# Column roll of an 8192 x 8192 matrix: two rows per engine and DMA in the first three eighths of the copy

## Chip, core and metric

The kernel runs on one core of a Trainium2 chip. The metric is the device time of one launch in microseconds (us); lower is better. Three timed runs of the kernel before gave 815.59, 817.35 and 817.82 us, median 817.35 us.

## The reference

```python
def setup_inputs():
    return {"x": np.random.randn(8192, 8192).astype(np.float32), "shift": 100}

def reference(x, shift):
    return np.roll(x, shift, axis=1)
```

Each row of 8192 float32 values (32 KiB) is rotated right by 100 columns. There is no arithmetic: 256 MiB are read and 256 MiB are written, and every output element is a copied input element. Column w of the output is column w - 100 of the input; the first 100 output columns come from the last 100 input columns.

## The kernel before

A row of the output is cut in two at column a = 256 (the shift 100 rounded up to 128, and one more 128). The columns from 256 on, 7936 values or 31,744 B of each row, are the body; the columns below 256 are the head.

**The body (L37 to L46)** goes from DRAM to DRAM with no stop on the chip. L34 and L35 view the 8192 rows as 128 blocks c of 64 rows; inside a block, engine index e (16 values) and row index j (4 values) name row 4e + j. One `dma_start` at L45 takes one block c and one j: 16 rows that lie four rows (128 KiB) apart, one for each of the 16 DMA engines, 496 KB in all. SP (`nc.sync`) starts at block 0 and goes up, j from 0 to 3. ACT (`nc.scalar`) starts at block 127 and goes down, j from 3 to 0. Both take a DMA in turn in the order of the program: the loop runs i from 0 to 63, so i is SP's block and 127 - i ACT's. In the last two rounds (i = 62 and 63) `parts` cuts every row in two halves, so that a DMA carries 248 KB.

After each i the name of its last DMA is put on the list `marks` (L46), 64 entries in all.

**The head (L63 to L97)** is done by POOL (`nc.gpsimd`) and DVE, in 16 tiles of 512 rows, four rows to each of 128 partitions. `fetch` (L72) issues a load from POOL and makes it wait for the landing of the fetch four before it in the list `chain`. A tile has three fetches: t, which holds 256 columns around the boundary between a row and the next for three of the four rows; and two smaller ones straight into h. DVE copies the two parts of t to their places in h (L87 and L90). When all fetches are issued, POOL issues the 16 stores of h (L94), 512 KB each. Store k is held until a DMA of the body has landed: the one in `marks` at 24 + 36k/15, rounded down, so the first store waits for i = 24 and the last for i = 60.

SP and ACT issue nothing but the body's DMAs. POOL's queue holds the fetches in order and behind them the stores. A body DMA adds 16 to one of eight semaphores, four of them SP's and four ACT's, which the tile framework hands out in turn; before it reuses one it waits for the DMA that used it last. The first four DMAs of a queue have no such wait.

Of the kernel before, what the change touches and what calls it, by code (L numbers as in the profile page):

```python
# [1 line left out]

# [4 lines left out]


@with_exitstack
def kernel(  # L10
    ctx: ExitStack,
    tc: tile.TileContext,
    x: bass.AP,
    shift: int,
    out: bass.AP,
):
    nc = tc.nc
    n_rows, n_cols = x.shape
    s = shift % n_cols
    a = -(-s // 128) * 128  # L20
    if 0 < a <= 384 and a + 128 <= n_cols:
        a += 128
    g = a - s
    P = nc.NUM_PARTITIONS
    engines = [nc.sync, nc.scalar]
    n_chunks = 16
    rows = n_rows // n_chunks

    xm = x.rearrange("(c e j) w -> c j e w", e=16, j=4)  # L34
    om = out.rearrange("(c e j) w -> c j e w", e=16, j=4)  # L35
    marks = []
    if a < n_cols:  # L37
        blocks = n_rows // 64
        mid = (a + n_cols) // 256 * 128
        for i in range(blocks // 2):  # L40
            parts = ((a, mid), (mid, n_cols)) if i >= blocks // 2 - 2 and a < mid else ((a, n_cols),)
            for j in range(4):
                for eng, c, q in ((engines[0], i, j), (engines[1], blocks - 1 - i, 3 - j)):
                    for lo, hi in parts:
                        ins = eng.dma_start(out=om[c, q, :, lo:hi], in_=xm[c, q, :, lo - s:hi - s])  # L45
            marks.append(getattr(ins, "ins", ins).name)  # L46
    if a == 0:
        return


    if a > 512:
        for i in range(n_chunks):
            r = slice(i * rows, (i + 1) * rows)
            nc.gpsimd.dma_start(out=out[r, :s], in_=x[r, n_cols - s:])
            if g > 0:
                nc.gpsimd.dma_start(out=out[r, s:a], in_=x[r, :g])
        return

    Q = 4  # L63
    n_st = n_rows // (P * Q)
    reads = ctx.enter_context(tc.tile_pool(name="reads", bufs=n_st))
    heads = ctx.enter_context(tc.tile_pool(name="heads", bufs=n_st))
    xt = x.rearrange("(k p q) c -> k p q c", q=Q, p=P)
    ot = out.rearrange("(k p q) c -> k p q c", q=Q, p=P)
    tiles = []
    chain = []  # L70

    def fetch(to, of):  # L72
        ins = nc.gpsimd.dma_start(out=to, in_=of, single_packet=True)  # L73
        ins = getattr(ins, "ins", ins)
        if len(chain) >= 4:
            tc.add_manual_dep(ins, chain[-4].name,
                              mybir.DependencyInfo(mybir.DependencyClass.Sync, mybir.DependencyReason.DATA))
        chain.append(ins)

    for k in range(n_st):  # L80
        t = reads.tile([P, Q - 1, a], x.dtype)
        h = heads.tile([P, Q, a], x.dtype)
        lead = bass.AP(tensor=x.tensor, offset=(k * P * Q + 1) * n_cols - s,
                       ap=[[Q * n_cols, P], [n_cols, Q - 1], [1, a]])
        fetch(t[:], lead)
        fetch(h[:, Q - 1, :s], xt[k, :, Q - 1, n_cols - s:])
        nc.vector.tensor_copy(h[:, :Q - 1, :s], t[:, :, :s])  # L87
        if g > 0:
            fetch(h[:, 0, s:], xt[k, :, 0, :g])
            nc.vector.tensor_copy(h[:, 1:, s:], t[:, :, s:])  # L90
        tiles.append(h)
    first, last = len(marks) * 3 // 8, len(marks) * 15 // 16
    for k, h in enumerate(tiles):
        ins = nc.gpsimd.dma_start(out=ot[k, :, :, :a], in_=h[:], single_packet=True)  # L94
        if marks and n_st > 1:
            tc.add_manual_dep(getattr(ins, "ins", ins), marks[first + (last - first) * k // (n_st - 1)],
                              mybir.DependencyInfo(mybir.DependencyClass.Sync, mybir.DependencyReason.DATA))  # L97


# [1 line left out]
_INS = ['x', 'shift']  # L101
_OUTS = [((8192, 8192), 'float32')]

_NUMBERS = {'shift': 100}


# [26 lines left out]
```

## Time and profile before

| | |
|---|---|
| median of three runs | 817.35 us |
| the profiled execution | 816.2 us |
| its span, first to last instruction | 814.4 us |
| body DMAs from SP and from ACT | 264 each: 248 of 496 KB, 16 of 248 KB |
| issue to landing, 496 KB | 12.7 us (median) |
| fetches of t, 384 KB, issue to landing | 29.5 us (median) |
| head stores, 512 KB, issue to landing | 21.1 us (median) |
| first and last head store issued | 327.7 and 779.4 us |
| last fetch issued | 281.5 us |

The span is what the profile covers; the device time is 1.8 us longer. In the queue lines q1 is SP's, q10 ACT's and q0 POOL's; the columns are packets, MB, and the time of the packets as a share of the span of 16 engines. GB/s counts each byte once, although a byte of the body is both read from and written to HBM. "Issue to landing" runs from the issue on the queue to the last engine's semaphore write. The lines of waits name who waited, for what, the total in us, the number of times and the longest. The clock column in the stretches is TensorE's and plays no part here.

### The profile page before, as it was taken

The numbers are of one execution on the slowest core, as the hardware profiler recorded it, in microseconds if no ns is written. First come the engines' busy times: TensorE is split into PE (matmuls) and PEld (weight loads), VectorE is DVE, ScalarE is ACT, GpSimd is POOL, SyncE is SP. The second block draws the span as 40 slices with busy tenths as digits, with TensorE's granted clock in tenths as the row PEclk, the third lists the DMA queues.
The fourth block names the chain that finished last, engine by engine and source line by source line (L and its number), as shares of the span: only waits on it lengthen the run. The fifth ranks groups of instructions, "written<-read, shape, count | busy, mean of one in ns | idle before, by whom it ended". The sixth has DMA issues, their size and how long they took to land.

```text
span 814.4 us, 689 instructions
## 1 busy us (share of the span) xinstructions
DVE 12.0 (1%) x32; POOL 41.2 (5%) x68
## 2 busy tenths in 40 slices
DVE  0000000000000000000000000000000000000000
POOL 1001001101001000000000000000000000000000
DMA  9999999999999999999999999999999999999998
GB/s 314 346 347 343 351 344 332 338 347 342 356 344 349 345 334 338 345 337 342 337 350 322 352 338 335 357 342 331 352 352 318 356 347 335 340 339 347 334 331 294
DMA packets 22277, 276.90 MB, mean 340 GB/s; under 512 B 9472, under 2 KB 9728, under 8 KB 13824
## 3 DMA queue, kind: packets, MB, share of 16 engines
q1 hardware_dynamic: 8448, 130.04, 46.8%
q10 hardware_dynamic: 8448, 130.04, 44.1%
q0 software_dynamic: 5376, 16.78, 8.1%
q14 instruction: 5, 0.04, 0.0%
HBM read 268.44 MB, written 268.44 MB: 659 GB/s over the span
## 4 chain that ended last, share of the span: by engine, by line
DMA 95%; ACTq 0%; issue 0%; POOLq 0%
DMA out_dram<-in_x_dram 95%; ACTq L45 0%; POOLq L128 0%; POOLq L94 0%
## 5 line engine op out<-in xcount | busy, mean ns | idle before, releaser
L94 POOL DMA_DIRECT2D out_dram<-h x16 | 11.4, 715 | 486.7 <-DMA out_dram<-in_x_dram 448.9
L73 POOL DMA_DIRECT2D h<-in_x_dram x32 | 17.5, 547 | 197.1 <-DMA t<-in_x_dram 165.0
L73 POOL DMA_DIRECT2D t<-in_x_dram x16 | 12.1, 759 | 54.9 <-DMA h<-in_x_dram 54.0
L87 DVE COPY h<-t 128x300 f32<-128x300 f32 x16 | 5.9, 367 | 287.3 <-DMA t<-in_x_dram 287.3
L90 DVE COPY h<-t 128x468 f32<-128x468 f32 x16 | 7.5, 468 | 0.0
L114 POOL MEMSET const-float32-0.0<- 128x1 f32 x1 | 0.1, 99 | 0.2 <-issue 0.2
L114 POOL MEMSET const-bfloat16-1.0<- 128x1 bf16 x1 | 0.1, 102 | 0.0
L114 POOL MEMSET const-float32-1.0<- 128x1 f32 x1 | 0.1, 99 | 0.0
L114 POOL MEMSET const-uint8-127<- 128x1 uint8 x1 | 0.1, 99 | 0.0
## 6 DMA issues: line engine op xcount, KB each, us to landing
out_dram<-in_x_dram SPq DMA_DIRECT2D x248, 496.0 KB, 12.7
out_dram<-in_x_dram ACTq DMA_DIRECT2D x248, 496.0 KB, 12.7
out_dram<-h POOLq DMA_DIRECT2D x16, 512.0 KB, 21.1
t<-in_x_dram POOLq DMA_DIRECT2D x16, 384.0 KB, 29.5
out_dram<-in_x_dram SPq DMA_DIRECT2D x16, 248.0 KB, 5.9
out_dram<-in_x_dram ACTq DMA_DIRECT2D x16, 248.0 KB, 5.9
h<-in_x_dram POOLq DMA_DIRECT2D x16, 78.0 KB, 24.3
h<-in_x_dram POOLq DMA_DIRECT2D x16, 50.0 KB, 21.2
```

Source lines behind the costliest of these rows:

```text
L73: ins = nc.gpsimd.dma_start(out=to, in_=of, single_packet=True)
L87: nc.vector.tensor_copy(h[:, :Q - 1, :s], t[:, :, :s])
L90: nc.vector.tensor_copy(h[:, 1:, s:], t[:, :, s:])
L94: ins = nc.gpsimd.dma_start(out=ot[k, :, :, :a], in_=h[:], single_packet=True)
L114: nc = _bacc.Bacc("TRN2", target_bir_lowering=False, num_devices=1)
```

## The change

For i below blocks * 3 // 16 = 24 (of 64) a DMA takes two values of j: its 16 engines each get two neighbouring rows, one after the other, 992 KB in all. There are then two DMAs of SP and two of ACT for an i, not four and four: 96 fewer over both queues. SP's rows keep their order (0 and 1, then 2 and 3). ACT takes the rows 2 and 3 of its block and then 0 and 1. `marks` still gets one entry for each i, and the rounds from i = 24 on, the head and its marks are as they were.

```diff
         for i in range(blocks // 2):
             parts = ((a, mid), (mid, n_cols)) if i >= blocks // 2 - 2 and a < mid else ((a, n_cols),)
+            if i < blocks * 3 // 16:
+                for j in (0, 2):
+                    for eng, c, q in ((engines[0], i, j), (engines[1], blocks - 1 - i, 2 - j)):
+                        ins = eng.dma_start(out=om[c, q:q + 2, :, a:].rearrange("j e w -> e j w"),
+                                            in_=xm[c, q:q + 2, :, a - s:n_cols - s].rearrange("j e w -> e j w"))
+                marks.append(getattr(ins, "ins", ins).name)
+                continue
             for j in range(4):
                 for eng, c, q in ((engines[0], i, j), (engines[1], blocks - 1 - i, 3 - j)):
                     for lo, hi in parts:
```

## The prediction

> **What bounds the kernel now.** I read the sections on slices and queues of the page first, then the chain, then the waits of SP's queue, then busy shares by stretch, then the single packet records of the trace.
>
> ```profile
> span 814.4 us, 689 instructions
> DMA  9999999999999999999999999999999999999998
> GB/s 314 346 347 343 351 344 332 338 347 342 356 344 349 345 334 338 345 337 342 337 350 322 352 338 335 357 342 331 352 352 318 356 347 335 340 339 347 334 331 294
> ...
> q1 hardware_dynamic: 8448, 130.04, 46.8%
> q10 hardware_dynamic: 8448, 130.04, 44.1%
> q0 software_dynamic: 5376, 16.78, 8.1%
> ...
> HBM read 268.44 MB, written 268.44 MB: 659 GB/s over the span
> ...
> DMA 95%; ACTq 0%; issue 0%; POOLq 0%
> ...
> out_dram<-in_x_dram SPq DMA_DIRECT2D x248, 496.0 KB, 12.7
> ```
>
> The 16 DMA engines are busy from end to end: the three queues add up to 99% of their time, and 95% of the chain is the copy from DRAM to DRAM. Nothing else matters unless it changes how fast these engines move bytes. q1 is SP's queue, q10 ACT's, q0 POOL's. One DMA gives each engine one row of 31,744 B and one 4-byte semaphore write: 264 DMAs x 16 engines x 2 = 8448 packets. The queues' 90.9% of 16 x 814.4 us is 11,845 us; over 8192 whole rows (248 + 8 DMAs, the 16 half ones counted as 8, x 16 x 2 queues) that is 1.44 us a row. In the packet records the fastest tenth of the rows takes 1.175 us and a semaphore write 0.009 us, the next packet starting 0.006 us after it. So about a fifth of a row's time is waiting for memory, and semaphore writes are next to nothing.
>
> The wait of SP's queue, with the fixed form of its 264 issues:
>
> ```profile
> SPq L45 <- DMA out_dram<-in_x_dram: 667.3, 259, 5.2
> ```
>
> ```profile
> L45 SPq DMA_DIRECT2D out_dram<-in_x_dram x264: 509/510/752, 0.7 to 807.0; - x132
> ```
>
> A queue issues one DMA in 814.4/264 = 3.08 us and lands it after 12.7 us: four are in flight, and the issue of the next waits for the landing of the one four before. The 16 half-size DMAs land after 5.9 us, about half, so the limit is four DMAs, whatever their bytes. SP spends 0.51 us of each 3.08 on issuing and waits for most of the rest: no engine starves for an issue.
>
> Shares of the engines by stretch (start:end, length, busy of DVE and POOL, clock, DMA share, GB/s):
>
> ```profile
> 20.00:160.00 140.00, 6.01 (x16) 14.73 (x24) 1.00 0.99 343
> 160.00:300.00 140.00, 6.01 (x16) 12.14 (x20) 1.00 0.99 346
> ...
> 320.00:780.00 460.00, 0.00 (x0) 11.35 (x16) 1.00 1.00 341
> 780.00:805.00 25.00, 0.00 (x0) 0.09 (x1) 1.00 0.92 333
> ```
>
> The reader is to see that the rate stays at 341 to 346 GB/s whether POOL fetches (to 300 us) or stores (after 327 us). The last line matters most: there half rows run, four in flight hold half the bytes, each byte carries twice the semaphore writes and the engines idle 8% of the time, and yet the rate falls by only (341 - 333)/341 = 2.3%. Engines that idle leave the others faster: most of the limit is shared. A per cent of engine time won or lost is worth about 2.3/8 = 0.29 of a per cent.
>
> **The change, part by part.** It covers i = 0 to 23: 96 DMAs of each queue become 48, of 992 KB each. In the profile these are the first 96/264 of the issues, to about 305 us.
>
> *Removed: 48 issues per queue.* 48 x 0.51 us = 24.5 us of SP and as much of ACT, both waiting anyway (667 us on SP): 0. Were that cover gone, it would cost those 24.5 us; it is a rival below.
>
> *Removed: 48 semaphore writes per queue and engine.* 2 x 48 x 0.009 = 0.9 us of engine time at most, 0.3 us at the shared rate of 0.29. I take -0.3.
>
> *A row now follows a row.* Following packets engine by engine through the records, the usual order is SP's row, ACT's row, SP's semaphore, ACT's semaphore, with a POOL packet between where there is one. Between 310 and 790 us, a row right after the two semaphores took 1.555 us in the mean and a row right after a row 1.462: 0.093 longer. Before 310 us the means are 1.495 and 1.277: 0.218. Half of these semaphore pairs go, 48 per engine, so 48 x 0.093 = 4.5 us to 48 x 0.218 = 10.5 us could be saved, if the semaphores cause the difference. Against that: the fastest tenth is 1.175 us after either, and the end stretch, with twice the semaphores per byte, is hardly slower. The near row is the end stretch, so I take 0 here; bounds 0 and -10.5.
>
> *Deeper queue.* Four DMAs in flight now hold eight rows per queue and engine, so a fast engine may run further ahead of the slowest before it starves. The idle per cent of 20 to 300 us is 0.01 x 280 = 2.8 us, at 0.29 worth 0.8 us: -0.8, bounds 0 and -2.8. Waits of SP and ACT become fewer and about twice as long (landing 12.7 to some 25 us); behind them on those queues stand only more copy DMAs, and the other three DMAs, six rows, keep the engines fed.
>
> *Back to one row at i = 24.* The permitted lead shrinks, and fast engines wait for slow ones. The nearest row is the end stretch, where the bytes in flight are halved too: 8% of 25 us idle = 2 us, at 0.29 worth 0.6 us. I take +0.6; bounds 0 and, if the fastest engine is a whole extra window ahead (4 rows of each queue, 8 x 1.44 = 11.5 us, half of it in the mean, nothing shared), +5.8.
>
> *ACT's row order.* Its blocks went 3, 2, 1, 0; now 2, 3, 0, 1. Same rows per block, so 0; no row here bounds it from below or above other than the spread of the slices, which the slow rival uses.
>
> *POOL's fetches.* Engines give q0 a packet per round in the records: two rounds per pair of rows now (rows, semaphores), three per two pairs after. A tile's fetches are 12 packets per engine (9 of data, 3 semaphores), six pairs, near the 285/16 = 17.8 us of before (5.5 pairs at 3.25 us). After, 12/1.5 = 8 pairs, 26 us: some 12 tiles fetched by 305 us, the last four at 18 us, the end near 375 us, not 300. All stores stand behind the fetches in POOL's order, so the first moves from 327.7 to about 380 us. Their marks are unchanged and come 30 us apart, while a store lands in 21 us, so two late stores catch up by 450 us. DRAM rows take the place of the late fetch bytes meanwhile: 0. Were the rows of a DMA one packet, fetches would last to about 450 us, the stores would still catch up long before the last mark at 779 us: 0 again.
>
> Sum: -0.3 - 0.8 + 0.6 = -0.5 us. The profiled execution took 816.2 us (span 814.4 plus 1.8 around it): 815.7. The median of the runs shown is 817.35, which would give 816.9. I put the forecast between, **816.3 us**.
>
> **Rivals.**
>
> *Faster: the engines, not the memory, set the pace* (30%). All of the idle per cent (2.8), the semaphore writes (0.9) and the read-after-semaphore term at its lower value (4.5) come off in full: 816.2 - 8.2 = 808.0; with only half the last two 810.7. For it: rows after rows are shorter in both stretches, and idling is larger in just the stretch that changes. Against it: the end stretch.
>
> *Slower: the wider lead costs memory time* (21%). Engines spread over eight rows of each queue instead of four, with reads and writes of more rows mixed, and the fifth of a row that is waiting grows. The place is the first 305 us; the price by the worst 20 us stretches inside it: those of 140 to 160 and 200 to 220 us ran at 337 and 335 against 344 for 20 to 305 us, so 305 x (344/336 - 1) = 7.3 us, 823.5. It decides once the stretch falls below about 341 GB/s. For it: slices vary between 318 and 357 with no change of work, so the arrangement in time matters. Against it: 3 to 20 us, when the engines have hardly drifted, already ran at 342.
>
> *Per-DMA cost is exposed* (3%). The 48 dropped issues of 0.51 us show on the end: 816.2 - 24.5 = 791.7. Against it: SP's 667 us of waiting. The Trainium skill, DMA: Bandwidth & Descriptors, section Rules for kernel authors, asks for DMAs of at least 1 MiB, and its Anatomy section puts a fixed 2.0 us on each; as an estimate from that page 48 x 2.0 = 96 us would go, about 720 us. This trace does not agree so far: at 496 KB its engines are already 99% busy, as four DMAs in flight hide such a cost.
>
> That the change fails to do what it says would be a DMA that runs on fewer engines; the leading dimension stays 16, as in the issues of before, so I give it nothing of its own.
>
> **How the numbers follow.** The forecast has 46%, its own range 813 to 820. About 0.3% (2.4 us) is what a measurement can tell from no change. Of the forecast's 46, 42 fall within that and 4 faster; the faster rivals add 30 and 3, the slower 21: faster 0.37, same 0.42, slower 0.21. The range reaches to the faster rival at its full price (808) and past the slower one's (823.5), to 825; what is left out is the exposed cost and the far ends of both.
>
> **What would show it.** q1 and q10 with 7680 packets each (768 semaphore writes fewer); a landing near 25 us for 992 KB; first store near 380 us; DMA share 1.00 and 341 to 348 GB/s up to 300 us; a dip in the slice after about 300 us below 2 us in engine time. A rate of 350 or more there means the faster rival, below 341 the slower. The forecast is wrong if semaphore writes hold up the reads behind them, or if the lead between engines, and not the shared limit, governs how long a row takes.

## The result, and the profile after

The changed kernel took 821.52 us (median of six runs, 819.13 to 823.41), the kernel before on the same chip 816.91 us (six runs, 815.23 to 817.82): a ratio of 1.0059, 95% interval 1.0044 to 1.0073. It is slower, by 4.6 us. The profiled execution took 819.13 us, the fastest of its six, with a span of 817.3 us, 2.9 us longer than before: the traces can account for these 2.9 us of the 4.6.

The page of the changed kernel (slices, queues, HBM, issues):

```profile
span 817.3 us, 593 instructions
...
GB/s 316 342 328 340 342 346 337 351 341 327 350 340 344 339 329 313 327 354 354 358 344 341 339 340 337 346 349 328 352 346 326 346 349 343 327 350 344 339 325 303
...
q1 hardware_dynamic: 7680, 130.04, 46.1%
q10 hardware_dynamic: 7680, 130.04, 43.7%
q0 software_dynamic: 5376, 16.78, 8.5%
...
HBM read 268.44 MB, written 268.44 MB: 657 GB/s over the span
...
out_dram<-in_x_dram SPq DMA_DIRECT2D x48, 992.0 KB, 25.7
```

The packets are those forecast, 768 fewer on each queue, and a 992 KB DMA lands after 25.7 us. The two body queues take 89.8% of 16 x 817.3 us = 11,743 us over 8192 rows, 1.434 us a row with its share of semaphore writes, where it was 1.446: a row costs no more than it did. The three queues add up to 98.3%, which leaves 13.9 us in which an engine is idle; before it was 99.0% and 8.1 us. The added time lies between the packets. Part of it shows in the 15th to 17th slice, at 329, 313 and 327 GB/s. The stretches of the two kernels (columns as in the prediction); first the changed one:

```profile
20.00:160.00 140.00, 3.76 (x10) 9.20 (x15) 1.00 0.98 340
160.00:300.00 140.00, 4.51 (x12) 10.83 (x18) 1.00 0.98 340
300.00:320.00 20.00, 0.75 (x2) 1.28 (x3) 1.00 0.87 304
320.00:360.00 40.00, 1.50 (x4) 4.42 (x7) 1.00 0.98 340
360.00:400.00 40.00, 1.50 (x4) 3.28 (x5) 1.00 1.01 356
```

The two stretches of the kernel before that answer to the dip:

```profile
300.00:320.00 20.00, 0.00 (x0) 0.00 (x0) 1.00 0.99 334
320.00:360.00 40.00, 0.00 (x0) 1.45 (x2) 1.00 1.00 340
```

At 300 to 320 us, just after the last two-row DMA is issued (296 us), the engines are busy 87% where they were 99%: (0.99 - 0.87) x 20 = 2.4 us of idle engines, and (1.00 - 0.98) x 40 = 0.8 us in the next stretch. The sum is 3.2 us. The share up to 300 us is lower too, 0.98 against 0.99, which is 2.8 us more; that these two parts together exceed the 2.9 us of span shows that idle time alone doesn't tell where time was lost. The bytes do.

Up to 300 us the counted rate is 340 GB/s, not 343 to 346, but less of it is POOL's fetches, whose bytes pass HBM once, where a byte of the body is both read and written. Before, fetches had about 8.39 MB / 300 us = 28 of 344.5 GB/s, so HBM carried 2 x 316.5 + 28 = 661; after, with twelve tiles of sixteen fetched by then, about 21 of 340, so 2 x 319 + 21 = 659. The memory is loaded as before. Counted in this way from the packet records, a byte of the body twice and one of POOL's once, the changed kernel is only 0.5 us of traffic behind at 300 us. From 300 to 320 us it moves 576 GB/s where it was 667, which costs 2.8 us at the mean of 659. It is 3.2 us behind at 400 us and still 3.2 at 780: what was lost was lost around the handover.

Who is late shows in the sixteen semaphore increments that the trace keeps for each DMA, one per engine. I take as the lag of a DMA its last increment minus the median one, averaged over the DMAs that land in a stretch:

```
                     20-60  60-120  120-180  180-240  240-300  300-320  320-360 us
before                 3.7     5.6      6.0      4.9      6.0      5.7      4.4 us
changed                4.8    13.4     16.6     16.5     16.5     13.5      6.9 us
```

It is not one engine alone. From 120 to 180 us the four latest engines land 6.8, 9.3, 12.7 and 16.6 us behind the median in the mean; from 180 to 300 us three do, by 6.3, 7.4 and 16.5, so that the last trails by another 9 us. The rest land within 2 us after the median. In the changed kernel the DMA that ends round 15 reaches the median engine 5 us earlier than before and the slowest one 6 us later. That is the theory the experiments set out to test: **lead**. Four DMAs in flight let the other engines run up to eight rows of each queue ahead of the slowest; when one-row DMAs return, the permitted lead halves and they stand still until the slowest have caught up. The runs were made on several chips; a ratio is always to the kernel before, run beside it on the same chip.

### The profile page after: what moved, and what is told of

Read it like the earlier page. It is cut to its first block, busy times and chain, and to the rows that moved or that the text cites. A ratio compares the mean times of both kernels' runs of the same rounds, so it can differ in the third digit from the quotient of the medians.

```text
span 817.3 us, 593 instructions
## 1 busy us (share of the span) xinstructions
DVE 12.0 (1%) x32; POOL 41.2 (5%) x68
## 2 busy tenths in 40 slices
DMA packets 20741, 276.90 MB, mean 339 GB/s; under 512 B 7936, under 2 KB 8192, under 8 KB 12288
## 3 DMA queue, kind: packets, MB, share of 16 engines
q0 software_dynamic: 5376, 16.78, 8.5%
## 4 chain that ended last, share of the span: by engine, by line
DMA 95%; ACTq 0%; issue 0%; POOLq 0%
DMA out_dram<-in_x_dram 95%; ACTq L45 0%; POOLq L135 0%; POOLq L101 0%
## 6 DMA issues: line engine op xcount, KB each, us to landing
out_dram<-in_x_dram ACTq DMA_DIRECT2D x48, 992.0 KB, 25.7
out_dram<-in_x_dram SPq DMA_DIRECT2D x48, 992.0 KB, 25.7
```

## The experiments

**Two DMAs in flight.** In the changed kernel each two-row DMA also waits for the one two before it on its queue (`lines` starts as two empty lists):

```diff
+                        line = lines[0] if eng is engines[0] else lines[1]
+                        raw = getattr(ins, "ins", ins)
+                        if len(line) >= 2:
+                            tc.add_manual_dep(raw, line[-2],
+                                              mybir.DependencyInfo(mybir.DependencyClass.Sync, mybir.DependencyReason.DATA))
+                        line.append(raw.name)
```

> Theory 'lead': while POOL fetches, one engine falls behind the other fifteen; the change lets these run eight rows per queue ahead, and they wait for it when the window narrows. Here two-row DMAs stay, but each waits for the one two before it on its queue, so four rows are in flight as in the kernel before. Lead expects the slowest engine within 6 us of the median engine at the end of the phase (changed kernel: 12), no dip at 300 to 320 us, and about 817 us, at most 2 us more if two DMAs in flight leave fast engines idle now and then. Rival 'form': the two-row DMA itself (half the semaphore writes, fewer turns for POOL's fetches, ACT's row order) costs the time; it expects the 821.5 us of the changed kernel.

Measured: 818.08 us against 816.49, ratio 1.0016 (1.0005 to 1.0027); the lag from 160 to 300 us is 5.3 us (16.5 in the changed kernel). Stretches of this kernel around the end of the phase:

```profile
160.00:300.00 140.00, 4.51 (x12) 11.03 (x18) 1.00 0.99 340
300.00:320.00 20.00, 0.75 (x2) 1.84 (x3) 1.00 1.01 348
320.00:360.00 40.00, 1.50 (x4) 2.54 (x4) 1.00 1.00 349
```

The dip is gone with the same two-row DMAs, semaphore writes and row order. Most of the loss is in the number of rows in flight; 0.16% is left over. In HBM traffic this profiled run is 0.4 us behind the kernel before at 400 us, where the changed kernel was 3.2; it loses its remaining time later, where the two programs issue the same DMAs.

**Three DMAs in flight.** The same with `>= 3` and `line[-3]`.

> Three two-row DMAs in flight per queue, six rows. Lead expects a value between: slowest engine some 8 to 9 us behind the median, 818 to 820 us. Form expects 821.5 us.

Measured: 819.39 us, ratio 1.0040 (1.0025 to 1.0055), a lag of 11.2 us from 160 to 300 us and a share of 0.96 at 300 to 360. Between, as lead has it; the lag was larger than expected.

**Four rows per DMA.**

```diff
-                for j in (0, 2):
-                    for eng, c, q in ((engines[0], i, j), (engines[1], blocks - 1 - i, 2 - j)):
...
+                for eng, c in ((engines[0], i), (engines[1], blocks - 1 - i)):
+                    ins = eng.dma_start(out=om[c, :, :, a:].rearrange("j e w -> e j w"),
+                                        in_=xm[c, :, :, a - s:n_cols - s].rearrange("j e w -> e j w"))
```

> Four rows per engine and DMA in the first three eighths, four DMAs and so sixteen rows in flight per queue. Lead expects the slowest engine 20 us or more behind the median near 300 us, a deeper dip after it, and 825 to 832 us. Form expects a further step of the size of the first or less, 822 to 824 us, with no larger gap between the engines needed.

Measured: 831.88 us, ratio 1.0188 (1.0175 to 1.0202), a lag of 37 us. Its stretches:

```profile
160.00:300.00 140.00, 3.76 (x10) 7.91 (x13) 1.00 0.98 337
300.00:320.00 20.00, 0.00 (x0) 1.28 (x2) 1.00 0.57 220
320.00:360.00 40.00, 2.26 (x6) 4.23 (x7) 1.00 0.84 293
```

Against the 0.99 and 1.00 of before, 0.42 x 20 + 0.16 x 40 = 14.8 us of idle engines stand against a span that is 831.1 - 814.4 = 16.7 us longer. In HBM traffic it is 1.9 us behind at 300 us and 15.7 at 340. The rows in flight per queue and the ratios go together: 4 (two in flight) 1.0016, 6: 1.0040, 8: 1.0059, 16: 1.0188.

**ACT's row order alone.** In the kernel before, ACT takes rows 2, 3, 0, 1 of its first 24 blocks: `(j ^ 2) if i < blocks * 3 // 16 else 3 - j` in place of `3 - j`.

> The kernel before, one row per DMA, with only ACT's row order of the change (2, 3, 0, 1) in its first 24 blocks. Lead expects the 816.9 us of the kernel before, within 1.5 us. A rival 'order' expects 820 to 822 us.

Measured: ratio 0.9998 (0.9990 to 1.0007). With one row per DMA the order costs nothing that can be told from zero.

**Without the head, one row and four rows.** `return` in place of `if a == 0: return`, in the kernel before and in the one with four rows.

> The kernel before without the head: POOL and DVE do nothing, the first 256 output columns are not written. It is the reference for the next run. At an unchanged rate 16.78 of 276.9 MB less give 816.5 x (1 - 16.78/276.9) = 767 us. If POOL's packets are what makes one engine lag, the slowest engine should land within 3 us of the median one (with the head 4 to 6); if an engine lags by itself, 4 to 6 us as before.

> Four rows per DMA in the first three eighths, and no head (its columns are not written). Theory 'POOL makes the lag': within 2 us of the same kernel with one row per DMA and no head, slowest engine under 10 us behind the median, no dip near 300 us. Theory 'an engine lags by itself': some 10 to 15 us above it, a lag of 30 us or more and a dip, as with the head.

Measured, on a chip where the kernel before took 828.34 us: 0.9655 (0.9635 to 0.9675) with one row, 0.9703 (0.9684 to 0.9721) with four. Without POOL's work the lag with four rows is 1.9 us from 160 to 300 us, and the share after 300 us stays at 1.00. With one row it is 5.0 us, as large as with POOL and not the 3 us at most that was expected if POOL made it: four engines land together, 4.2 to 5.0 us behind the median. So a lag of 5 us needs no POOL; one that grows with the rows in flight does. The second run is still 0.5% above the first, with neither such a lag nor a dip: 321 GB/s from 20 to 160 us against 328, while the engines land within 2 to 4 us of each other. The stretches, one row and then four (without DVE's column, as it does nothing here):

```profile
20.00:160.00 140.00, 0.00 (x0) 1.00 1.00 328
```

```profile
20.00:160.00 140.00, 0.00 (x0) 1.00 0.99 321
```

So the four-row form has a cost besides the lag, whose cause I did not find; lead alone had expected 2 us at most, and it was 3.7. The kernel without the head saved 3.5%, not the 6% of its share of the counted bytes; more on that at the end.

**Two rows later.** `if blocks * 3 // 16 <= i < blocks * 3 // 8`: rounds 24 to 47, where POOL stores.

> Two rows per DMA not in rounds 0 to 23 but in 24 to 47, where POOL stores and does not fetch; all else as in the kernel before. If the lag needs the fetches: 816.5 us, within 1.5. If an engine lags in any stretch: 820 to 822 us, with a lag of 12 us or more between 330 and 600 us and the dip after it.

Measured, on that same chip: 1.0008 (0.9997 to 1.0018), a lag of 7.2 us from 420 to 600 us and a share of 0.94 from 620 to 640 us. The same number of two-row DMAs costs nothing that can be told from zero where POOL only stores.

**Three one-row DMAs in flight** in the first three eighths of the kernel before, by the same extra wait.

> The kernel before with three one-row DMAs in flight per queue, not four, in its first three eighths. Lead expects the lag of the slowest engine to fall from 5 or 6 us to about 4 there. If the smaller lead were all that counted, about 815.5 us; if fast engines starve with so few bytes in flight, 817 to 820 us with a DMA share below 0.99 in the stretch.

Measured: 1.0004 (0.9989 to 1.0019), lag 2.6 us from 160 to 300 us, share 0.99 to 1.00. A smaller lead than that of the kernel before brings nothing, and three rows are enough to feed the engines. So no version here that does the whole work beats the kernel before.

**Four rows again, and without the fetches.** The second kernel keeps the stores and stores zeros: `nc.vector.memset(h[:], 0.0)` in place of the three fetches and the two copies.

> The kernel with four rows per DMA once more, so that the next runs stand beside it on the same chip. Ratio to the kernel before 1.0188 on another chip; here 1.012 to 1.022, with one engine 30 us or more behind the median near 240 to 300 us.

> Four rows per DMA, POOL's stores kept, its fetches left out (DVE fills the head's tiles with zeros, so the first 256 output columns are zeros). Theory 'the fetches make the lag': the lag before 300 us stays under 5 us, no dip after it, and the time lies below that of the kernel before by part of the fetches' 8.39 MB, 0 to 20 us. Theory 'an engine lags whatever POOL does': a lag of 30 us and a dip to a share below 0.8, 10 us or more above what it would be otherwise.

Measured on one chip: with fetches 1.0154 (1.0074 to 1.0233; the runs behind it took from 823 to 834 us), without 0.9884 (0.9860 to 0.9908). First the stretches with fetches, then without:

```profile
300.00:320.00 20.00, 0.75 (x2) 1.30 (x2) 1.00 0.63 241
320.00:360.00 40.00, 1.51 (x4) 4.21 (x7) 1.00 0.88 309
```

```profile
20.00:160.00 140.00, 0.00 (x0) 0.00 (x0) 1.00 0.99 325
160.00:300.00 140.00, 0.00 (x0) 0.00 (x0) 1.00 1.00 327
300.00:320.00 20.00, 0.00 (x0) 0.11 (x1) 1.00 0.98 332
320.00:360.00 40.00, 0.00 (x0) 1.44 (x2) 1.00 1.00 343
```

The lag from 160 to 300 us is 20 us with the fetches (27 from 240 to 300 us, where 30 or more was expected) and 5 without, where it had 16 rows to grow in. It is the fetches that hold engines back beyond those 5 us. They are several here too: with the fetches the last but one lands only 2 us before the last.

**Which engine.** Four rows per DMA, with small loads of the first 16, 15, 8 and 7 rows on both queues:

```diff
+                if i in width:
+                    k = width[i]
+                    for eng in engines:
+                        probe = probes.tile([k, 128], x.dtype)
+                        eng.dma_start(out=probe[:], in_=x[i * 64:i * 64 + k, :128])
```

> Four rows per DMA, and in eight rounds of the phase a small load of 16, 15, 8 or 7 rows (8, 7.5, 4 or 3.5 KB) on each of SP's and ACT's queues, which lands when the engines that it uses have come so far. If a load of n rows goes to the first n engines and the engine that lags is always the last one, the loads of 16 rows land 20 us or more later after their issue than those of 15; if it is the eighth, those of 16, 15 and 8 are late and those of 7 early; if another one or a changing one lags, the four show no such step.

The issues of this kernel (KB each, median us to landing where the trace has it):

```profile
probe<-in_x_dram SPq DMA_DIRECT2D x2, 8.0 KB, 37.1
probe<-in_x_dram ACTq DMA_DIRECT2D x2, 8.0 KB, 35.2
probe<-in_x_dram SPq DMA_DIRECT2D x2, 7.5 KB, 28.0
probe<-in_x_dram ACTq DMA_DIRECT2D x2, 7.5 KB, 34.4
```

There is no step of 20 us. The loads of 7 rows are late as well: the last of their seven engines adds its increment 22 to 34 us after the issue and 20 to 29 us after the first of the seven, in all four of them. (Loads of less than 16 rows have one more increment 0.4 to 0.7 us after the issue, which is left out here.) With two loads of a kind on each queue, and in-flight places taken by the probes themselves, this says that at least one late engine is among the seven that serve the smallest load, and not which. Whether it is always the same stays open. The kernel took 824.93 us in its one run, against 816.18 before.

**Two rows for longer.** `if i < blocks * 3 // 8`: rounds 0 to 47.

> Two rows per DMA in the first three quarters (rounds 0 to 47), not three eighths; the window narrows near 610 us, some 230 us after the last fetch. Lead, with the cost paid where the window narrows while an engine lags: the lag shrinks under the stores, the dip at 300 to 320 us is gone, a smaller one may come near 610 us, and the ratio to the kernel before is 1.000 to 1.005, not above the 1.0059 of the changed kernel. If each two-row DMA costs something by itself, twice as many cost twice as much: 1.010 to 1.013.

Measured: 823.02 us against 816.27, ratio 1.0085 (1.0069 to 1.0101): outside both expectations. Its stretches:

```profile
300.00:320.00 20.00, 0.75 (x2) 1.84 (x3) 1.00 1.00 338
...
600.00:620.00 20.00, 0.00 (x0) 0.25 (x1) 1.00 0.94 333
620.00:640.00 20.00, 0.00 (x0) 0.72 (x1) 1.00 0.91 324
```

The dip has moved from 300 us to where the window now narrows. But the lag did not shrink under the stores as I had assumed: it is 17 us from 120 to 320 us and still 12 from 420 to 600, after the last fetch at 389 us. The dip's idle time is 0.06 x 20 + 0.09 x 20 = 3.0 us, the span 819.5 - 814.4 = 5.1 us longer. In HBM traffic the dip costs 1.8 us; the other 3.2 us were lost little by little before 600 us, for which I have no cause.

**Is there a cost of the form itself?** Without fetches, one row and two rows; and two in flight in rounds 0 to 47.

> The kernel before without the fetches (zeros are stored in the head's columns, as with four rows): the reference for the next run. Four rows without fetches had 0.9884 of the kernel before; here 0.983 to 0.988.

> The changed kernel without the fetches (zeros in the head's columns). Lead, with the fetches as the cause of the lag: the same as the run with one row and no fetches, within 0.15 per cent, and no lag above 6 us. If the two-row form costs something by itself, fetches or not: 0.2 to 0.5 per cent more than that run.

> Two-row DMAs, two in flight per queue, in rounds 0 to 47, not 0 to 23. If what was left over with two in flight (1.0016) belongs to the stretch with the fetches, 1.0016 again, within 0.0012; if each two-row DMA costs something by itself, about 1.0032.

Measured on one chip: 0.9822 (0.9805 to 0.9839), 0.9834 (0.9814 to 0.9853), and 1.0007 (0.9995 to 1.0019). Two rows without fetches cost 0.12% more than one row, inside both intervals, with a lag of 5.4 us from 160 to 300 us. Their share falls to 0.93 at 300 to 320 us, yet the rate there is 335 GB/s where it was 334 with one row, so a short idle share need not cost bytes. The first ratio is a little below the range expected. Twice as many two-row DMAs with two in flight cost no more than half as many. A cost of the two-row form comes out at 0.1 to 0.2% and can't be told from zero by these runs. With four rows the pair without the head showed 0.5%, and without the fetches 0.9884 stands against 0.9822 with one row, 0.6%, though on different chips.

## Why the prediction was wrong

The forecast was no change (816.3 us). The time is 821.52: outside the forecast's own range of 813 to 820, inside the whole range of 808 to 825, and slower by more than the 0.3% that a measurement can tell.

*The bound, the issues, the semaphore writes, the row after a row, ACT's order.* Right within what the runs can tell. HBM moves 657 GB/s where it moved 659. From 20 to 300 us, where the semaphore writes were halved, a row took 1.360 us in the mean and 1.349 before: fewer semaphores did not shorten it. ACT's order alone gave 0.9998.

*Back to one row at i = 24.* **This step failed**, by its size: +0.6 us was taken, from the end stretch and the shared rate of 0.29; the profile has 3.2 us of idle engines there, over the 2 us that the prediction gave as its sign, and 2.8 us of traffic that was not moved, and the median time grew by 4.6. The discount was the mistake. At the handover the engines were 13% less busy (0.98 before, 0.86 now, by the packet records from 300 to 320 us) and HBM carried 14% less: nothing was shared. The rows that did run there took 1.355 us in the mean, 1.487 before, but their fastest tenth still 1.175, so the engines still at work did not make up for those that stood still. In the end stretch no engine is far behind, the last landing 2.0 us after the median, and 8% of idle time cost 2.9% of HBM traffic (665 to 646 GB/s; the 2.3% of the prediction mixes in the stores, whose bytes pass HBM once). The upper bound, +5.8 us with nothing shared, was the better model.

*Deeper queue.* The other half of the same failure: -0.8 us for idle time won back. The share up to 300 us went from 0.99 to 0.98 instead, the traffic up to there stayed that of before within 0.5 us, and the median engine's lead, 5 us at round 15, was handed back at the narrowing. I took the lead of the engines as random; in fact the last trails by 16.5 us, in a window of 25.7 us, from 120 to 300 us. With the lead cut to four rows 1.0016 of 1.0059 were left, and the 0.09% between the runs with two in flight over 24 and over 48 rounds says how far such a rest can be read.

*POOL's fetches.* Right in time and wrong in weight. The last fetch was issued at 370.3 us (forecast 375) and the first store at 370.9 (380), and the changed kernel falls no further behind in traffic after 400 us, so the later stores cost nothing that shows:

```profile
370.34 0.54 POOL L80 DMA_DIRECT2D h<-in_x_dram  x1 [2.12 <-DMA h<-in_x_dram]
370.91 1.48 POOL L101 DMA_DIRECT2D out_dram<-h  x2
```

But I counted the fetches only as bytes and turns. They are also what sets engines back: 37 and 20 us of lag with them at four rows, 5 without.

*The slower rival* (823.5 us) named the wider lead, and that is the cause; its mechanism, rows that take longer in memory, is not what happened: they took 0.8% longer up to 300 us, at the same HBM traffic. Its sign, a rate below 341 GB/s, came true with 340 and misled, since the counted rate falls when less of it is fetches. The Trainium skill, DMA: Bandwidth & Descriptors, section Latency and other measured facts, says that engines 7 and 15 are usually slower and puts it, as a guess, down to the descriptor rings of DMAs issued from GpSimd. That the lag beyond 5 us comes with POOL's fetches and goes with them agrees (16.5 against 5.4 us with two rows); that it is those two engines no run here shows, and three or four trail in the changed kernel.

*Per-DMA cost is exposed.* It did not show: 48 issues fewer on each queue saved nothing. The Trainium skill, DMA: Bandwidth & Descriptors, section Rules for kernel authors, asks for at least 1 MiB per DMA for most bandwidth. That did not pay here: 496, 992 and 1984 KB gave 1, 1.0059 and 1.0188. The 2.0 us that the prediction takes from the Trainium skill stand there for DMAs issued from GpSimd; the body's are issued by SP and ACT.

Open are: which engines lag and by what in the fetches, the 3.2 us that the run with two rows for longer lost ahead of its dip, and the cost of four rows without a lag.

## What to carry to other kernels

Where a queue allows a fixed number of DMAs in flight, a larger DMA also widens the lead that fast engines may take over a slow one. With the engines already 99% busy that lead bought nothing here, and it was paid back at full price where the window narrowed; price such a point by the slowest engines, not by the mean rate. Look at the spread of a DMA's sixteen increments, not only at its landing, before changing the size of transfers next to other traffic.

## What the runs showed of the hardware

The limit looks like memory traffic rather than moved bytes. Leaving out the fetches, 8.39 of 276.9 MB or 3.0% of the counted bytes, saved 1.8% (ratio 0.9822), near the 8.39 of 536.9 MB = 1.6% that they are of all HBM reads and writes. The body alone ran at 332 to 333 GB/s there, which is 2 x 332.5 = 665 GB/s of HBM traffic, against the 661 with fetches worked out above on another chip:

```profile
20.00:160.00 140.00, 0.00 (x0) 0.00 (x0) 1.00 1.01 333
160.00:300.00 140.00, 0.00 (x0) 0.00 (x0) 1.00 1.00 332
```

Counted rates of stretches with a different mix of traffic can't be compared directly. Leaving out the whole head points the same way: 16.78 MB are 6.1% of the counted bytes and 3.1% of the HBM traffic, and 3.5% was saved.

And beside POOL's fetches the latest of the 16 DMA engines stayed behind the median by 5 us with four rows in flight per queue, 11 with six, 16.5 with eight, and 37 and 20 with sixteen, with several engines late at once.
